# The first norm's sum of squares moved from GpSimd to ScalarE, and the first operands read from PSUM

## The chip, the cores and the metric

One Trainium2 chip, one core of it. The metric is the time of one execution on the device in microseconds (us); lower is better. A core has TensorE (matrix multiplication), VectorE and GpSimd (elementwise work), ScalarE (elementwise functions) and SyncE, which here only issues DMA transfers. In the profile they are PE (PEld for its weight loads), DVE, POOL, ACT and SP.

## The reference

One layer of a decoder for 512 tokens of 1024 features, all in float32: a half-step gated feed-forward, two attention mixers with a gated merge, a second half-step feed-forward, a last norm. The change lies in the first feed-forward alone:

```
def _rmsnorm(x, g):
    xf = x.astype(jnp.float32)
    y = xf * lax.rsqrt(jnp.mean(xf * xf, axis=-1, keepdims=True) + RMS_EPS)
    return (y * g.astype(jnp.float32)).astype(x.dtype)

def _swiglu(x, w_gate, w_up, w_down):
    return (jax.nn.silu(x @ w_gate) * (x @ w_up)) @ w_down
...
    h = x
    ...
        h = h + FFN_HALF * _swiglu(_rmsnorm(h, norm_ffn1[i]), ffn1_gate[i], ffn1_up[i], ffn1_down[i])
```

`x` is 512 x 1024, the gate and up weights are 1024 x 2816, the down weights 2816 x 1024.

## The kernel before, in words

**Operands in two parts.** Every large product is made of three matmuls of 128x128 weights with 512 moving columns. A float32 operand is split into a high part, rounded by ScalarE (`uh` for activations, `whi` for weights), and a low part, what the rounding left, subtracted by VectorE (`ul`, `wlo`). The product is whi·uh + whi·ul + wlo·uh, summed in one bank of PSUM.

**Layout.** Activations lie with features on partitions: `h[:, d]` is the d-tile, 128 features by 512 tokens; there are eight, numbered 0 to 7 here. The input comes with tokens on partitions (`x`, four blocks of 128 tokens), so TensorE first transposes four 128x128 blocks of each tile into a bank `tp`. There are two such banks, used in turn.

**The norm's factor is applied late.** The matmuls take h times the gain, without the token's factor 1/sqrt(mean of squares). The factor, `r_b`, is worked out beside them, and multiplies the products afterwards (`swiglu`). `norm_in` makes uh and ul of a tile and calls `square`, in which GpSimd adds the tile's squares to `sqacc`. `norm_col` sums `sqacc` over partitions by matmuls with a column of ones and turns the sums into factors (`nv`, `ny`, `nb`, `rcol`); `norm_rows` spreads them over partitions into `r_b`.

**The start.** For the first two f-tiles (128 columns of gate and of up each), four products run along while the input arrives: `begun` holds four PSUM banks, named o, s, acc and o by the profile, and `begin(f, m, d)` adds tile d's three matmuls to one of them (f the f-tile, m gate or up). `x_in(d)` makes a tile: transposes, the copy to `h[:, d]` on VectorE, `norm_in`, and the split of the tile's rows of these first weights (`w_in0`) into `W.hi` and `W.lo`, 128x512. Each engine works its instructions in the order of the code; that order is written by hand here: x_in(0), x_in(1), then in turn the twelve matmuls of tile d and x_in(d + 2). At the end come tiles 6 and 7, with nine matmuls of tile 6 (three banks) before those of tile 7.

**After it.** Later weights come in blocks of 128 columns, eight k-tiles deep, into four slots; `W.next` splits a block two ahead of its use (`high` on ScalarE, `low` on VectorE). Blocks 0, 1, 2 go to the slots that the start used. `mm3` is a block's 24 matmuls; at three quarters of the first block's it calls `col` (that is, `norm_col`), in the second's `rows`.

Of the kernel before, what the change touches and what calls it, by code (L numbers as in the profile page):

```python
# [16 lines left out]
D = 1024  # L17
# [21 lines left out]
def parts(x):  # L39
    """x as three parts of eight bits, whose products with 16-bit integers are exact in float32, and a rest."""  # L40
    out = []
    for _ in range(3):
        m, e = math.frexp(x)
        c = math.ldexp(round(m * 256), e - 8)
        out.append(c)
        x -= c
    return out + [x]
# [11 lines left out]
class Weights:  # L59
    """Streams 128-column blocks of weights from DRAM and splits them into a high and a low part."""  # L60
# [49 lines left out]
    def prep_pair(self):  # L110
        """The next two blocks, by halves of their rows."""
# [16 lines left out]
    def next_pair(self):  # L128
        """Two blocks side by side, as [128, 2, 8, 128]."""
        i = self.pos  # L130
        assert i % 2 == 0
        self.prep(i + 1 + self.AHEAD)
        self.pos += 2
        s = i % self.SLOTS
        return self.hi[:, s:s + 2], self.lo[:, s:s + 2]
# [10 lines left out]
def cols(w, width, r0, nk, c0, n):  # L146
    """Rows r0..r0+128*nk, columns c0..c0+n of a [rows, width] matrix, as [128, nk, n]."""
# [3 lines left out]
class Ring:  # L151
    """n buffers, used in turn."""
# [16 lines left out]
class Task:  # L169
    """A few instructions of one engine: emit() issues them. It takes a buffer of some rings and gives back others."""  # L170
# [6 lines left out]
class Schedule:  # L177
    """Orders tasks by a list schedule: whatever can start first, and the lower rank first where several can."""
# [7 lines left out]
    def add(self, us, emit, after=(), take=(), give=(), rank=0):  # L186
        """us: the engines that can do it, with their estimated microseconds."""
# [40 lines left out]
def layer(ctx, tc, a, out):  # L228
# [27 lines left out]
    # ---- the order in which the weights are used  # L256
# [45 lines left out]
    # ---- constants  # L302
# [46 lines left out]
    def rope_tables(p):  # L349
        """Cosines and sines of position x inverse frequency, for any int32 position: the angle is brought to  # L350
        [-pi, pi] by multiples of 2 pi and of 65536 that are exact in parts."""
# [51 lines left out]
    # ---- norms  # L403
    def norm_in(d, norm):
        """The d-tile of the normed input without the token's factor, in two parts; its sum of squares."""
# [13 lines left out]
    def norm_col():  # L419
        """1 / sqrt(mean of squares + eps), with tokens on partitions."""  # L420
        ps = tbank()
        for t in range(4):
            mm(ps[:, 0, t:t + 1], sqacc[:, t * 128:(t + 1) * 128], ones[:, :1], True, True)
        v = temp.tile([128, 4], F32, name="nv", bufs=1)
        vector.tensor_scalar(v, ps[:, 0, :4], 1.0 / D, EPS, op0=OP.mult, op1=OP.add)
# [19 lines left out]
    # ---- feed-forward  # L445
# [23 lines left out]
    def ffn(after, begun=(), side=None, finish=None):  # L469
        """begun: gates and ups of the first f-tiles; after(d): when a d-tile is done; side: small pieces of other  # L470
        work, one for each f-tile; finish: the last third's products with the down weights, in another way."""
        norm = {}

        def col():
            norm["col"] = norm_col()
# [29 lines left out]
    # ---- first feed-forward  # L505
    hd = tc.dram_tile([KD, 128, S], F32, name="hd")

    with pool("h1") as h_pool, pool("temp1", 2) as temp, pool("start") as start:
# [22 lines left out]
        def rows_in(n):  # L531
            """The first n rows, as columns."""
# [8 lines left out]
        def x_in(d):  # L541
# [3 lines left out]
            vector.tensor_copy(h[:, d], flat(ps))  # L545
            norm_in(d, 0)
            src = w_in0[:, d].rearrange("p m (f c) -> p f m c", f=2)
            hi, lo = (w[:, :, d].rearrange("p (f m) c -> p f m c", f=2) for w in (W.hi, W.lo))
            scalar.copy(hi, src)
            vector.tensor_tensor(lo, src, f32(hi), op=OP.subtract)  # L550

        def begin(f, m, k):
            s = 2 * f + m
            mm(begun[f][m], W.hi[:, s, k], uh[:, k], k == 0, False)
            mm(begun[f][m], W.hi[:, s, k], ul[:, k], False, False)
            mm(begun[f][m], W.lo[:, s, k], uh[:, k], False, k == KD - 1)
# [4 lines left out]
        for d in range(KD - 2):  # L561
            for f in range(2):
                for m in range(2):
                    begin(f, m, d)
            x_in(d + 2)
        W.load(2)
        load_rest()
        for f, m, d in ((0, 0, 6), (0, 1, 6), (1, 0, 6), (0, 0, 7), (0, 1, 7), (1, 0, 7), (1, 1, 6), (1, 1, 7)):
            begin(f, m, d)
# [20 lines left out]
        ffn(to_mix, begun, side_work())  # L590

    # ---- mixers
    with ExitStack() as mixing:
# [16 lines left out]
        # places that are used for other things before the attention needs them  # L610
# [11 lines left out]
        # -- the first projection, as the input gets ready; keys and values that will be compressed  # L622
# [29 lines left out]
        # -- everything up to the merge: a list schedule of small tasks  # L652
# [14 lines left out]
        def either(us):  # L667
            """An elementwise step on SBUF that VectorE does in us microseconds, or GpSimd."""
# [4 lines left out]
        def prepare(first, n):  # L673
            """Tasks that split the blocks first.., by halves of their rows."""
# [35 lines left out]
        class Bank:  # L710
            """A PSUM bank, taken when its first task is issued."""
# [6 lines left out]
        def project(done):  # L718
            """256 columns of the input projection with tokens on partitions; done(t0, bank, task) for each bank."""
# [17 lines left out]
        def rope(src, t0, nt, nh):  # L737
            """src [128, nt, nh, 64] turned by the tables of the tokens of t0.., and times the token's factor: two
            parts, to be added."""
# [10 lines left out]
        class Turned:  # L750
            """What rope leaves, between its task and the next ones."""
# [13 lines left out]
        # where a rotated or transposed operand is complete  # L765
# [655 lines left out]
```

## Time and profile before

| | |
|---|---|
| median of 3 timed runs | 1151.49 us (1151.38 to 1151.9) |
| span of the profiled execution, first to last instruction | 1146.2 us |
| median less that span | 5.3 us |
| TensorE busy | 1119.1 us, 98% of the span |
| VectorE busy | 661.4 us, 58% |
| ScalarE busy | 436.9 us, 38% |
| GpSimd busy | 151.6 us, 13% |
| granted TensorE clock, mean | 0.997 of full speed |

The profile gives a span for the profiled execution and no other time of it; what lies around the span is taken from the median. The shares are means over stages with different limits: TensorE is busy for 98% of the span, but for 31 of the first 40 us (4.95 in the first ten, 26.33 in the next thirty).

### The profile page before, as it was taken

Reading aid. Unit: us, or ns where it says so; the run is one execution under the profiler, and the core shown is the slowest. Engines: PE = TensorE matmul, PEld = TensorE weight load, DVE = VectorE, ACT = ScalarE, POOL = GpSimd, SP = SyncE. Lnnn points to the kernel's source line nnn. Section 1 sums busy time; section 2 is a strip of 40 time slices with the busy share of each in tenths; the row PEclk is TensorE's granted clock in tenths of the full one; section 3 lists DMA queues with packets and bytes.
Section 4 is the critical chain, followed back from the end, with each engine's and each line's share of the span. In section 5 each row is a group of like instructions: output and inputs, shape, how many; then the busy total and the mean of one; then the engine's idle time right before and its main releaser. Section 6 shows DMA issues by size and latency. Waiting matters only on the chain.

```text
span 1146.2 us, 14637 instructions
## 1 busy us (share of the span) xinstructions
PE 1119.1 (98%) x5591; PEld 940.1 (82%) x5591; DVE 661.4 (58%) x1227; ACT 436.9 (38%) x850; POOL 151.6 (13%) x152
## 2 busy tenths in 40 slices
PE   7999999999999999999999899999999999999997
PEld 5788888888888899888888688888888888888875
DVE  6665336443446689999889644565443354433453
ACT  3333123221233356767777533323232132222432
POOL 5300000000004321422121222241000000000001
PEclk9999999999999999999999999999999999999999
DMA  7233333333324533242211255433333333333221
GB/s 226 74 111 92 95 96 89 108 99 108 88 82 130 156 88 98 74 112 72 59 38 37 82 149 147 138 92 111 110 100 97 97 91 94 109 93 92 74 74 74
DMA packets 198287, 113.34 MB, mean 99 GB/s; under 512 B 4996, under 2 KB 191944, under 8 KB 198216
## 3 DMA queue, kind: packets, MB, share of 16 engines
q1 hardware_dynamic: 197416, 111.33, 34.0%
q8 instruction: 44, 0.72, 0.3%
q10 hardware_dynamic: 800, 1.07, 0.3%
q14 instruction: 27, 0.22, 0.1%
HBM read 105.83 MB, written 6.55 MB: 98 GB/s over the span
## 4 chain that ended last, share of the span: by engine, by line
PE 86%; DVE 8%; ACT 1%; issue 1%; POOLq 0%; DVEq 0%; ACTq 0%
PE acc L250 31%; PE s L250 27%; PE o L250 24%; DVE wlo L97 2%; PE tp L1224 2%; DVE s L1130 1%; DVE pts L1239 1%; PE tp L250 1%; DVE osum L1267 0%; DVE pbuf L1161 0%; PE tp L850 0%; DVE h L501 0%; DVE pbuf L1159 0%; PE tp L1345 0%; ACT whi L93 0%
## 5 line engine op out<-in xcount | busy, mean ns | idle before, releaser
L97 DVE TENSOR_TENSOR wlo<-raw,whi 128x1024 fp32r<-128x1024 f32 (+3 forms) x221 | 242.6, 1127 | 28.4 <-ACT whi L93 27.3
L93 ACT CAST whi<-raw 128x1024 fp32r<-128x1024 f32 (+3 forms) x223 | 189.8, 890 | 132.7 <-PE acc L250 53.1
L250 PE MATMUL acc<-uh,whi 128*128 128x512 f32 x296 | 116.9, 395 | 0.0
L250 PE MATMUL acc<-uh,wlo 128*128 128x512 f32 x296 | 115.8, 391 | 0.0
L250 PE MATMUL acc<-ul,whi 128*128 128x512 f32 x296 | 115.4, 390 | 0.0
L250 PE MATMUL s<-uh,whi 128*128 128x512 f32 x280 | 109.5, 391 | 0.0
L250 PE MATMUL s<-ul,whi 128*128 128x512 f32 x280 | 109.2, 390 | 0.0
L250 PE MATMUL s<-uh,wlo 128*128 128x512 f32 x280 | 109.2, 390 | 0.0
L250 PE MATMUL o<-uh,wlo 128*128 128x512 f32 x256 | 100.6, 393 | 3.7 <-DVE wlo L550 3.7
L250 PE MATMUL o<-uh,whi 128*128 128x512 f32 x256 | 101.0, 394 | 0.0
L250 PE MATMUL o<-ul,whi 128*128 128x512 f32 x256 | 100.0, 391 | 0.0
L253 ACT CAST G<-g 128x512 fp32r<-128x512 f32 x44 | 27.3, 621 | 186.7 <-DVE g L466 186.7
L250 PE MATMUL acc<-G,whi 128*128 128x512 f32 x280 | 87.5, 394 | 0.0
L250 PE MATMUL s<-G,whi 128*128 128x512 f32 x228 | 70.3, 390 | 0.0
L250 PE MATMUL o<-G,whi 128*128 128x512 f32 x228 | 70.2, 389 | 0.0
L250 PE MATMUL acc<-whi,uh 128*128 128x256 f32 x224 | 64.7, 289 | 2.1 <-DVE v L809 2.1
L250 PEld LDWEIGHTS acc<-uh,wlo 128*128 128x128 f32 x296 | 55.6, 188 | 12.2 <-DVE wlo L97 0.4
L250 PE MATMUL acc<-wlo,uh 128*128 128x256 f32 x224 | 63.6, 284 | 1.6 <-DVE wlo L97 1.6
L250 PEld LDWEIGHTS acc<-uh,whi 128*128 128x128 f32 x296 | 55.8, 188 | 10.8 <-issue 0.2
L250 PEld LDWEIGHTS acc<-ul,whi 128*128 128x128 f32 x296 | 55.7, 188 | 10.6
L462 ACT ACTIVATE s<-z 128x512 f32<-128x512 f32 x44 | 27.9, 633 | 95.2 <-DVE z L460 95.2
L250 PE MATMUL acc<-whi,ul 128*128 128x256 f32 x224 | 63.3, 283 | 0.0
(291 smaller groups left out, 2140.2 us busy)
## 6 DMA issues: line engine op xcount, KB each, us to landing
raw<-in_ffn_gate_dram SPq DMA_DIRECT2D x42, 512.0 KB, 4.0
raw<-in_ffn_up_dram SPq DMA_DIRECT2D x42, 512.0 KB, 5.0
raw<-in_ffn_down_dram SPq DMA_DIRECT2D x38, 512.0 KB, 4.5
raw<-in_w_in_dram SPq DMA_DIRECT2D x32, 512.0 KB, 4.6
raw<-in_w_out_dram SPq DMA_DIRECT2D x8, 512.0 KB, 4.2
raw<-in_ffn_down_dram SPq DMA_DIRECT2D x8, 384.0 KB, 4.1
zd<-turn_a SPq DMA_DIRECT2D x9, 256.0 KB, 2.1
z<-zd SPq DMA_DIRECT2D x9, 256.0 KB, 2.8
```

The costliest lines, as they stand in the source:

```text
L93: self.nc.scalar.copy(self.place(i)[0][:, k0:k1], self.raw[i][:, k0:k1])
L97: engine.tensor_tensor(lo, self.raw[i][:, k0:k1], f32(hi), op=OP.subtract)
L250: tensor.matmul(out, lhsT, rhs, start=start, stop=stop)
L253: scalar.copy(hi, src)
L462: scalar.activation(s, z, AF.Silu)
L1130: vector.tensor_tensor_reduce(b.view[:, j], b.view[:, j], u.mask, 1.0, u.least(hd), OP.add, OP.min, u.m[:, hd:hd + 1])
L1224: tensor.transpose(ps[:w, hd], u.p[:, hd, kb * w:kb * w + w], ident)
L1239: vector.tensor_tensor(p.lo, flat(b.ps)[:w], f32(p.hi), op=OP.subtract)
```

## The change

In the first feed-forward, the sum of squares is no longer taken from `h` on GpSimd but from the input `x`, with tokens on partitions, by four ScalarE activations (Square, with the sum of each row), one for each block of 128 tokens. `col_of` turns those sums into factors; the matmuls with a column of ones fall away for this norm. `uh` and `ul` are made from the transposed tile in PSUM, and the copy to `h` follows them. The order of the matmuls of `begin` is by operand: first whi·uh for all banks, then whi·ul, then wlo·uh. For tiles 6 and 7 the first f-tile's two banks come first, then the other two. In tile 0 the weights are rounded ahead of uh.

```diff
     def norm_col():
         ps = tbank()
         for t in range(4):
             mm(ps[:, 0, t:t + 1], sqacc[:, t * 128:(t + 1) * 128], ones[:, :1], True, True)
+        return col_of(ps[:, 0, :4])
+
+    def col_of(sums):
         v = temp.tile([128, 4], F32, name="nv", bufs=1)
-        vector.tensor_scalar(v, ps[:, 0, :4], 1.0 / D, EPS, op0=OP.mult, op1=OP.add)
+        vector.tensor_scalar(v, sums, 1.0 / D, EPS, op0=OP.mult, op1=OP.add)
...
-            norm["col"] = norm_col()
+            norm["col"] = norm_col() if sums is None else col_of(sums)
...
         def x_in(d):
             ps = tbank()
             for t in range(4):
                 tensor.transpose(ps[:, t], x[:, t, d * 128:(d + 1) * 128], ident)
-            vector.tensor_copy(h[:, d], flat(ps))
-            norm_in(d, 0)
+            g = gains[:, 0, d:d + 1]
             src = w_in0[:, d].rearrange("p m (f c) -> p f m c", f=2)
             hi, lo = (w[:, :, d].rearrange("p (f m) c -> p f m c", f=2) for w in (W.hi, W.lo))
-            scalar.copy(hi, src)
-            vector.tensor_tensor(lo, src, f32(hi), op=OP.subtract)
-
-        def begin(f, m, k):
-            s = 2 * f + m
-            mm(begun[f][m], W.hi[:, s, k], uh[:, k], k == 0, False)
-            mm(begun[f][m], W.hi[:, s, k], ul[:, k], False, False)
-            mm(begun[f][m], W.lo[:, s, k], uh[:, k], False, k == KD - 1)
+            if d == 0:
+                scalar.copy(hi, src)
+            scalar.activation(uh[:, d], flat(ps), AF.Identity, scale=g)
+            if d:
+                scalar.copy(hi, src)
+            if d == 0:
+                vector.tensor_tensor(lo, src, f32(hi), op=OP.subtract)
+            vector.scalar_tensor_tensor(ul[:, d], flat(ps), g, f32(uh[:, d]), op0=OP.mult, op1=OP.subtract)
+            if d:
+                vector.tensor_tensor(lo, src, f32(hi), op=OP.subtract)
+            vector.tensor_copy(h[:, d], flat(ps))
+
+        sums0 = start.tile([128, 4], F32, name="sums0")
+        x_sq = start.tile([128, D], F32, name="x_sq")
+
+        def sum_squares(t):
+            scalar.activation(x_sq, x[:, t], AF.Square, accum_out=sums0[:, t:t + 1])
+
+        PAIRS = [(f, m) for f in range(2) for m in range(2)]
+
+        def begin(pairs, k):
+            for n in range(3):
+                for f, m in pairs:
+                    s = 2 * f + m
+                    w = (W.hi, W.hi, W.lo)[n][:, s, k]
+                    mm(begun[f][m], w, (uh, ul, uh)[n][:, k], k == 0 and n == 0, k == KD - 1 and n == 2)
 
         x_in(0)
         x_in(1)
         vector.tensor_copy(ident_r, ident)
         for d in range(KD - 2):
-            for f in range(2):
-                for m in range(2):
-                    begin(f, m, d)
+            begin(PAIRS, d)
             x_in(d + 2)
+            if d >= 2:
+                sum_squares(d - 2)
         W.load(2)
         load_rest()
-        for f, m, d in ((0, 0, 6), (0, 1, 6), (1, 0, 6), (0, 0, 7), (0, 1, 7), (1, 0, 7), (1, 1, 6), (1, 1, 7)):
-            begin(f, m, d)
+        for pairs, d in ((PAIRS[:2], 6), (PAIRS[:2], 7), (PAIRS[2:], 6), (PAIRS[2:], 7)):
+            begin(pairs, d)
...
-        ffn(to_mix, begun, side_work())
+        ffn(to_mix, begun, side_work(), sums=sums0)
```

VectorE's order at tiles 2 and 3, before (the number behind a name tells buffers apart; `tp_173` and `tp_198` are the transposed tiles 2 and 3):

```order
L545 COPY h_108<-tp_173 128x512
L408 SCALAR_TENSOR_TENSOR ul_75<-h_108,cols_c_86,uh_74 128x512
L550 TENSOR_TENSOR wlo_71<-w_in0_112,whi_70 128x4x128
L545 COPY h_108<-tp_198 128x512
L408 SCALAR_TENSOR_TENSOR ul_75<-h_108,cols_c_86,uh_74 128x512
L550 TENSOR_TENSOR wlo_71<-w_in0_112,whi_70 128x4x128
```

The same place in the changed kernel, where `tp_171` and `tp_193` are tiles 2 and 3:

```order
L558 SCALAR_TENSOR_TENSOR ul_75<-tp_171,cols_c_86,uh_74 128x512
L560 TENSOR_TENSOR wlo_71<-w_in0_112,whi_70 128x4x128
L561 COPY h_108<-tp_171 128x512
L558 SCALAR_TENSOR_TENSOR ul_75<-tp_193,cols_c_86,uh_74 128x512
L560 TENSOR_TENSOR wlo_71<-w_in0_112,whi_70 128x4x128
L561 COPY h_108<-tp_193 128x512
```

The copy has moved from the head of a tile to its end, and ul has another source.

ScalarE's order in the changed kernel for tiles 6 and 7 and the first blocks of later weights (before, the same rows without the two Squares):

```order
L553 ACTIVATE uh<-tp,cols_c 128x512
L555 CAST whi<-w_in_112 128x4x128
L567 ACTIVATE x_sq,sums_136<-x 128x1024
L553 ACTIVATE uh<-tp,cols_c 128x512
L555 CAST whi<-w_in_112 128x4x128
L567 ACTIVATE x_sq,sums_136<-x 128x1024
L93 CAST whi<-raw 128x1024 x4
```

A Square stands behind each of tiles 4 to 7, the last of them ahead of the rounding of block 0.

TensorE's order at tiles 6 and 7, before: the first three rows are tile 6's for the first bank, the last three tile 7's for the same bank.

```order
L250 MATMUL o_132<-uh_74,whi_70 128x512
L250 MATMUL o_132<-ul_75,whi_70 128x512
L250 MATMUL o_132<-uh_74,wlo_71 128x512
L250 MATMUL s_133<-uh_74,whi_70 128x512
L250 MATMUL s_133<-ul_75,whi_70 128x512
L250 MATMUL s_133<-uh_74,wlo_71 128x512
L250 MATMUL acc_134<-uh_74,whi_70 128x512
L250 MATMUL acc_134<-ul_75,whi_70 128x512
L250 MATMUL acc_134<-uh_74,wlo_71 128x512
L250 MATMUL o_132<-uh_74,whi_70 128x512
L250 MATMUL o_132<-ul_75,whi_70 128x512
L250 MATMUL o_132<-uh_74,wlo_71 128x512
```

The same place in the changed kernel, six rows of tile 6 and six of tile 7:

```order
L250 MATMUL o_132<-uh_74,whi_70 128x512
L250 MATMUL s_133<-uh_74,whi_70 128x512
L250 MATMUL o_132<-ul_75,whi_70 128x512
L250 MATMUL s_133<-ul_75,whi_70 128x512
L250 MATMUL o_132<-uh_74,wlo_71 128x512
L250 MATMUL s_133<-uh_74,wlo_71 128x512
L250 MATMUL o_132<-uh_74,whi_70 128x512
L250 MATMUL s_133<-uh_74,whi_70 128x512
L250 MATMUL o_132<-ul_75,whi_70 128x512
L250 MATMUL s_133<-ul_75,whi_70 128x512
L250 MATMUL o_132<-uh_74,wlo_71 128x512
L250 MATMUL s_133<-uh_74,wlo_71 128x512
```

Six matmuls of tile 6 stand ahead of tile 7's first, where nine did, and each operand is asked for two matmuls at a time. The other twelve of the two tiles follow.

## Rows read from the trace of the kernel before

**Rows 1.** The page's first line.

```profile
span 1146.2 us, 14637 instructions
```

**Rows 2.** Chain that ended last, 0 to 70: start us, us, engine, tile, line.

```profile
39.02 4.08 PE s L250 x18
```

**Rows 3.** Waits, 0 to 60: who waited for whom, us in total, times, longest.

```profile
PEld o L250 <- DVE wlo L550: 6.4, 7, 1.5
```

**Rows 4.** Timeline: start us, us, engine, line, operation, out<-in, [idle before <-releaser].

```profile
11.58 0.48 PE L250 MATMUL o<-uh,whi 128*128 128x512 f32 x1
...
13.77 1.61 POOL L417 TENSOR_TENSOR sqacc<-sqacc,turn_a 128x512 f32<-128x512 f32 x1
...
14.16 1.77 DVE L550 TENSOR_TENSOR wlo<-w_in,whi 128x512 fp32r<-128x512 f32 x1
...
14.77 0.48 PE L250 MATMUL o<-uh,whi 128*128 128x512 f32 x1
...
15.86 0.68 DVE L545 COPY h<-tp 128x512 f32<-128x512 f32 x1
15.99 0.50 PE L250 MATMUL o<-uh,wlo 128*128 128x512 f32 x1 [0.51 <-DVE wlo L550]
...
30.64 0.48 PE L250 MATMUL o<-uh,whi 128*128 128x512 f32 x1
```

**Rows 5.** VectorE's groups, 10 to 36: count | busy us, mean ns | idle before, releaser.

```profile
L550 DVE TENSOR_TENSOR wlo<-w_in,whi 128x512 fp32r<-128x512 f32 x7 | 12.4, 1770 | 0.0
L408 DVE SCALAR_TENSOR_TENSOR ul<-h,cols_c,uh 128x512 fp32r<-128x512 f32 x7 | 6.1, 874 | 5.5 <-ACT uh L407 5.5
```

**Rows 6.** VectorE's groups, 0 to 10.

```profile
L550 DVE TENSOR_TENSOR wlo<-w_in,whi 128x512 fp32r<-128x512 f32 x1 | 0.7, 677 | 0.0
```

**Rows 7.** ScalarE's groups by form, whole span.

```profile
L549 ACT CAST whi<-w_in 128x512 fp32r<-128x512 f32 x8 | 4.8, 604 | 0.0
...
L443 ACT COPY r_b<-tp 128x512 f32<-128x512 f32 x3 | 1.8, 587 | 27.4 <-PE tp L250 27.4
```

**Rows 8.** ScalarE's groups by form, 1100 to 1146 (L1377 Square, L1389 Identity).

```profile
L1377 ACT ACTIVATE z<-o_t 128x512 f32<-128x512 f32 x8 | 5.1, 632 | 19.0 <-DVE o_t L1375 19.0
L1389 ACT ACTIVATE o_t<-o_t,fcol 128x512 f32<-128x512 f32 x4 | 2.9, 724 | 6.5 <-DVE fcol L1387 6.5
...
L1377 ACT ACTIVATION_READ_ACCUMULATOR z<-o_t 128x1 f32 x8 | 1.5, 185 | 0.0
```

**Rows 9.** Timeline, tile 7's low part and the blocks behind it.

```profile
35.78 0.50 PE L250 MATMUL o<-uh,wlo 128*128 128x512 f32 x1 [1.19 <-DVE wlo L550]
35.80 4.08 ACT L93 CAST whi<-raw 128x1024 fp32r<-128x1024 f32 x4 [2.16 <-issue]
...
36.88 3.50 DVE L97 TENSOR_TENSOR wlo<-raw,whi 128x1024 fp32r<-128x1024 f32 x3 [1.16 <-ACT whi L93]
...
38.86 0.39 PE L250 MATMUL s<-uh,whi 128*128 128x512 f32 x1
```

**Rows 10.** Timeline, around the matmuls with ones.

```profile
42.71 0.39 PE L250 MATMUL s<-uh,wlo 128*128 128x512 f32 x1
...
43.75 0.49 PE L250 MATMUL s<-uh,whi 128*128 128x512 f32 x1
```

**Rows 11.** Timeline, the start.

```profile
1.44 1.28 ACT L407 ACT_TABLE_LOAD   x1 [1.44 <-PEq L1409]
...
6.25 0.60 ACT L549 CAST whi<-w_in 128x512 fp32r<-128x512 f32 x1
...
6.41 1.09 PE L544 MATMUL tp<-ident,x 128*128 128x128 f32 x4 [1.55 <-DMA x<-in_x_dram]
...
7.14 0.78 PE L250 MATMUL o<-uh,whi 128*128 128x512 f32 x1
```

**Rows 12.** Tile w_in, the first gate weights' DMA, issued at 1.28.

```profile
DMA to landing us min/median/max: 2.8/2.8/2.8
```

**Rows 13.** Busy us by stretch (count); last columns granted clock, DMA share, GB/s.

```profile
645.00:646.00 1.00, 1.00 (x4) 0.81 (x4) 0.28 (x1) 0.58 (x1) 0.95 (x1) 0.50 0.00 0
```

More of the change, by code (lines that the diff above doesn't have):

```diff
@@ L467, in swiglu, with ffn @@
         split(G[:, j], G[:, 8 + j], g)
-    def ffn(after, begun=(), side=None, finish=None):
+    def ffn(after, begun=(), side=None, finish=None, sums=None):
         norm = {}
         def col():
-            norm["col"] = norm_col()
+            norm["col"] = norm_col() if sums is None else col_of(sums)
         def rows():
@@ L1064, in layer @@
         class Unit:
+            pass
         def nsa_units(g, order=range(4)):
```

## The prediction

> **What bounds the kernel now.** The profiled execution spans 1146.2 us [rows 1]; the timed runs have their median at 1151.49, so 5.3 us lie outside the span, and I carry them over unchanged. I read the chain of waits first. From 35.7 us on it is TensorE almost without a break, in stretches such as 18 matmuls in 4.08 us, 0.227 us for each [rows 2]. So whatever TensorE wins or loses early moves everything behind it, unless something later has a clock of its own. The list of waits of the first 60 us then says where TensorE is not yet the bound: its weight loads waited seven times, 6.4 us together, for the low part wlo of the first weights, which VectorE makes [rows 3]. The timeline of tiles 1 to 7 shows how [rows 4]. From the first matmul of tile 1 (11.58) to that of tile 2 (14.77) is 3.19 us: twelve matmuls and four transposes without a stall. Then tile 2's third matmul stands until 15.99. From 14.77 to 30.64, the first matmul of tile 6, four tiles take 15.87 us, 3.97 each.
>
> Why 3.97? VectorE is one loop: copy h (0.68), wait for ScalarE's uh, which reads that copy (0.80), ul (0.87), wlo (1.77), next copy. In the timeline the copy for tile 3 begins at 15.86, where wlo of tile 2 ends [rows 4]. And wlo is long: 1770 ns for each of seven [rows 5], but 677 ns for the one before 10 us [rows 6]. GpSimd is in its 1.61 us addition into sqacc when the long one starts at 14.16; that addition ends at 15.38, and wlo 0.55 us later [rows 4]. So I read wlo as held up by that addition, and the loop as made of three things that the change touches.
>
> **What the change does, part by part.** *GpSimd's fifteen instructions (one product, seven products, seven additions) go.* Nobody else waits for GpSimd there except the first normalization. wlo then should cost its undisturbed 0.68. Bounds: 0.68 [rows 6] and, if GpSimd is not the cause, 1.77 [rows 5]. I take 0.68.
>
> *uh and ul read PSUM, the copy h comes last.* ScalarE no longer waits for VectorE. uh from PSUM has no row; nearest are ScalarE's 587 ns copy of a bank to r_b [rows 7] and the 724 ns of an Identity with a scale column from SBUF [rows 8]; I take 0.72. ul from PSUM has no row either; I take today's 0.87 [rows 5]. VectorE per tile, with the copy of 0.68 [rows 4], is then 0.87 + 0.68 + 0.68 = 2.23 us, against the 3.19 that TensorE needs; ul could double and still fit. The bank of the transposes is held until the copy, but the next transposes into it come two tiles later. ScalarE per tile is 0.72 + 0.60 = 1.32 [rows 7].
>
> *Four Squares of 128x1024 on ScalarE, one behind each of tiles 4 to 7.* Two rows of 128x512 bound one from above: 2 x 0.632 + 0.185 for reading the accumulator = 1.45 [rows 8]; below, a single one with its read, 0.82. I take 1.45. ScalarE then needs 2.77 a tile, still under 3.19, so a Square may take up to 1.87 and stay hidden. What hides it is TensorE's own work. What waits behind the last Square is the rounding of weight block 0.
>
> Does Square need other tables than Identity? The change's instruction order has one table load at the start and none around the Squares, and in the last 46 us of today's span Square runs beside Identity [rows 8], with no table load among ScalarE's groups. The Trainium skill, "ScalarE: Activation LUTs", section "What ACT_TABLE_LOAD costs", puts every switch to another set at about 2.66 us, and its section "Table sets: the hidden batching unit" says that cheap functions stand in every set, without naming Square among them. No run here shows that figure; the trace has 1.28 us for a load [rows 11]. If two loads went with each Square, that page's price would make an estimated 1163; the sum below has none.
>
> *The steady tiles.* With both engines under 3.19, four periods of 3.97 become 3.19: 15.87 - 12.76 = 3.11 us won.
>
> *Tiles 6 and 7.* Tile 7's transposes are still issued just before tile 6's first matmul, so tile 7 is made in the shadow of tile 6's share. Before, that share was nine matmuls, and tile 7's third matmul still came only at 35.78; from 30.64 to block 0's first matmul at 38.86 went 8.22 us for 24 matmuls [rows 4, 9]. Now six matmuls (1.36 us) go first, then tile 7's, by operand: uh and whi are due 0.72 + 0.60 and some 0.2 of handing over after the transposes, so TensorE waits some 0.3; ul and wlo (0.87 + 0.68 behind uh, 2.3 in all) are due as two pairs of matmuls are done, 2.3 to 2.6. 24 x 0.227 = 5.45, plus 0.3, makes 5.75: 2.47 us won. Bounds of the wait: 0 and 0.6.
>
> *Block 0 behind it.* Today its rounding starts at 35.80, as tile 7's wlo ends, four take 4.08 on ScalarE, and three subtractions 3.50 on VectorE [rows 9]. In the new order it stands behind the last Square, about 1.6 + 1.45 = 3.1 us after tile 7's transposes; 1.02 of rounding and 1.17 of subtraction end at 5.3 to 5.5. TensorE wants the rounded part at 5.75 and the low part two matmuls later, at 6.2. It fits with some 0.7 us to spare, so I charge nothing; if the cover goes, each us beyond costs one.
>
> *The sum over partitions on TensorE.* The matmuls with a column of ones stood between two matmuls at 42.71 and 43.75 [rows 10]: 1.04 in place of 0.227, 0.81 us won. The rest of that chain (power, products, r_b) starts earlier; SyncE's queue keeps its order.
>
> *The grouping by operand.* Every matmul loads its weights as before; a group of four gives ul and wlo two more steps of time. I cost it at nothing.
>
> *The start.* Now the first table load waits for the first gate weights, issued at 1.28 and landed 2.8 us later [rows 12], at 4.1; plus 1.28, 0.60, 0.72 gives uh at 6.7, before tile 1's transposes, which wait for x until 6.41, let the first matmul go at 7.14 [rows 11]. When the up weights land no row says, but the cast that needs them began at 6.25 [rows 11]: at worst uh is 0.5 late. I take 0, bounds -0.15 (a gap between the first two matmuls) and +0.5.
>
> **Sum:** 3.11 + 2.47 + 0.81 = 6.4 us. The span goes to 1139.8, the time to **1145.1** (-0.56%).
>
> **Rivals.** *wlo stays at 1.77,* because something other than GpSimd stretches it. Against it stands the short one [rows 6]. VectorE then needs 0.87 + 1.77 + 0.68 = 3.32 a tile, 0.13 over TensorE, 0.5 in four tiles, and tile 7's low part comes 1.1 later: 1146.7.
>
> *Late start,* up weights at 6.25: 1145.6.
>
> *A later wait that goes or comes.* At 645 to 648 us three windows of 1 us ran at granted clock 0.50, four matmuls each [rows 13], the lower of the two levels (1.2 GHz), after a stretch of short pieces of attention. If the shifted timeline spares it, 1.5 us more are won: 1143.6. A second one would give 1146.6.
>
> *ScalarE becomes the bound through longer Squares,* without tables: beyond 1.87 each, four times the excess is lost. At 2.9, 4.1 us would go, and 1149.2 is left, a gain of 0.2%, which is about what a measurement of this kernel can tell from no change.
>
> *Square and Identity take turns in the tables.* Two loads of 1.28 [rows 11] make a Square 1.45 + 2.57 = 4.0. Tiles 5 to 7 and block 0 each come 4.0 - 1.87 = 2.15 late, 8.6 in all, of which about 1.4 is cover (tile 5's operands are ready that much ahead of need): 7.2 lost, 1152.3, slower than before; from 1.5 us a switch on it is slower by over 0.2%. The instruction order, with one load, and the end of today's span [rows 8] speak against it. The Trainium skill's price for a switch, on the page named above, lies beyond that point.
>
> **Chances.** The forecast 0.65; late start 0.12; wlo unchanged 0.10; the clock stretch spared 0.05; longer Squares 0.05; tables 0.03. The low end is the spared stretch with 0.3 for the spread of runs, 1143.3; the high end wlo unchanged with the same, 1147.0; both reach over the bounds of the start and of tile 7's wait. What lies outside is the last two cases and mishaps that I did not think of. Faster by over 0.2%: 0.92; within: 0.05; slower: 0.03.
>
> **What the changed profile would show.** No GpSimd work before the power step; all wlo of the first eight tiles near 0.68; first matmuls of tiles 2 to 6 each 3.19 apart, with the first of tile 6 near 27.5; block 0's first matmul near 33.3; no matmul with ones and sqacc between 42 and 44 less the shift; Squares of 1.2 to 1.45 with no table load beside them. The prediction is wrong if tiles still come over 3.4 apart, if ScalarE turns up as the releaser of TensorE's waits in tiles 5 to 7 for more than 1 us, if block 0 waits for its rounding, or if the 5 to 6 us won by 40 us are not there any more at the end.

## The result, and the profile after

The changed kernel took 1142.88 us (median of 4 runs, 1142.62 to 1143.16), the kernel before 1151.43 us beside it (4 runs, 1147.91 to 1151.9): ratio 0.9929, 95% interval 0.9915 to 0.9943. The direction was right; the time lies 0.4 us below the range's low end and 2.2 us below the forecast. The same kernel, run again later (e5 below), took 1146.55 us (7 runs, 1142.94 to 1146.66). Both are times of one program, and most of this text is about why they differ.

The page's first line and its busy times answer to [rows 1]:

```profile
span 1141.3 us, 14617 instructions
...
PE 1117.3 (98%) x5583; PEld 939.8 (82%) x5583; DVE 652.8 (57%) x1227; ACT 440.9 (39%) x858; POOL 132.1 (12%) x137
```

The profiled execution took 1143.02 us, 1.7 us more than its span. That is the first thing that does not fit the prediction, which put 5.3 us outside the span.

TensorE's timeline, the first matmuls of tiles 0, 1, 2, 6 and 7 and of block 0 (start, duration, in brackets the idle time before and who ended it), beside [rows 4, 9, 11]:

```profile
8.07 0.80 PE L250 MATMUL o<-uh,whi 128*128 128x512 f32 x1 [0.62 <-ACT uh L553]
...
10.37 0.63 PE L250 MATMUL s<-ul,whi 128*128 128x512 f32 x1
10.80 0.63 PE L250 MATMUL acc<-ul,whi 128*128 128x512 f32 x1
...
13.04 0.48 PE L250 MATMUL o<-uh,whi 128*128 128x512 f32 x1
...
16.23 0.48 PE L250 MATMUL o<-uh,whi 128*128 128x512 f32 x1
...
29.08 0.48 PE L250 MATMUL o<-uh,whi 128*128 128x512 f32 x1
...
30.61 0.50 PE L250 MATMUL o<-uh,whi 128*128 128x512 f32 x1
...
34.86 0.39 PE L250 MATMUL s<-uh,whi 128*128 128x512 f32 x1
```

From 16.23 to 29.08 four tiles take 12.85 us, 3.21 each, where they took 15.87: 3.02 won. From tile 6 to block 0 it is 5.78 where it was 8.22: 2.44 won. But tile 0 starts at 8.07 instead of 7.14, and from there to tile 1 it is 4.97 instead of 4.44 (11.58 - 7.14), since from one matmul to the next it is 0.4 us or more eight times, not six, as from 10.37 to 10.80: 0.93 + 0.53 = 1.46 lost. In the trace of before the slow pace ended with these two:

```profile
9.43 0.57 PE L250 MATMUL s<-uh,wlo 128*128 128x512 f32 x1
9.84 0.39 PE L250 MATMUL acc<-uh,whi 128*128 128x512 f32 x1
```

With the ones matmuls' 0.81, 3.02 + 2.44 + 0.81 - 1.46 = 4.81, against 1146.2 - 1141.3 = 4.9 between the two spans.

ScalarE's timeline shows why tile 0 is late, beside [rows 11]:

```profile
5.52 1.28 ACT L552 ACT_TABLE_LOAD   x1 [5.52 <-DMA w_in<-in_ffn_up_dram]
6.81 0.62 ACT L552 CAST whi<-w_in 128x512 fp32r<-128x512 f32 x1
7.34 1.26 ACT L553 ACTIVATE uh<-tp,cols_c 128x512 fp32r<-128x512 f32 x2
```

The table load stood at 1.44 before. Now the first activation in ScalarE's order is the cast of the weights, the load stands in front of it, and what the load waits for is the up weights' DMA, until 5.5.

VectorE's groups from 11 to 36 us (count | busy us, mean ns | idle before, releaser), beside [rows 5]:

```profile
L561 DVE COPY h<-tp 128x512 f32<-128x512 f32 x7 | 4.8, 685 | 0.0
L558 DVE SCALAR_TENSOR_TENSOR ul<-tp,cols_c,uh 128x512 fp32r<-128x512 f32 x6 | 4.5, 751 | 8.9 <-ACT uh L553 8.9
L560 DVE TENSOR_TENSOR wlo<-w_in,whi 128x512 fp32r<-128x512 f32 x6 | 4.1, 682 | 0.0
```

ScalarE's groups of the first 45 us, beside [rows 7, 8]:

```profile
L553 ACT ACTIVATE uh<-tp,cols_c 128x512 fp32r<-128x512 f32 x8 | 5.4, 687 | 11.1 <-PE tp L547 11.1
...
L567 ACT ACTIVATE x_sq<-x 128x1024 f32<-128x1024 f32 x4 | 4.3, 1064 | 0.0
...
L552 ACT ACT_TABLE_LOAD x1 | 1.3, 1283 | 5.5 <-DMA w_in<-in_ffn_up_dram 5.5
L567 ACT ACTIVATION_READ_ACCUMULATOR x_sq<-x 128x1 f32 x4 | 0.8, 189 | 0.0
```

wlo is 682 ns instead of 1770, a Square with its read 1.25 us, and there is one table load. Of the waits of the first 60 us (us in total, times, longest), the 6.4 us of [rows 3] are gone. These remain of the weight loads' waits for high and low parts; the middle one is at 58.5 us, in a later block, and the last is tile 7's:

```profile
PEld o L250 <- ACT uh L553: 1.0, 1, 1.0
...
PEld acc L250 <- DVE wlo L97: 0.4, 1, 0.4
PEld o L250 <- ACT whi L555: 0.3, 1, 0.3
```

### The profile page after: what moved, and what is told of

It reads as the page before. It is cut to its first block, busy times and chain, and to the rows that moved or that the text cites. A ratio compares the mean times of both kernels' runs of the same rounds, so it can differ in the third digit from the quotient of the medians.

```text
span 1141.3 us, 14617 instructions
## 1 busy us (share of the span) xinstructions
PE 1117.3 (98%) x5583; PEld 939.8 (82%) x5583; DVE 652.8 (57%) x1227; ACT 440.9 (39%) x858; POOL 132.1 (12%) x137
## 4 chain that ended last, share of the span: by engine, by line
PE 88%; DVE 8%; issue 1%; ACT 1%; DMA 0%; SPq 0%; POOLq 0%; DVEq 0%; ACTq 0%
PE acc L250 32%; PE s L250 28%; PE o L250 25%; DVE wlo L97 2%; PE tp L1244 2%; DVE s L1150 1%; DVE pts L1259 1%; PE tp L250 0%; DVE osum L1287 0%; DVE pbuf L1181 0%; PE tp L870 0%; DVE h L504 0%; DVE pbuf L1179 0%; DMA w_in<-in_ffn_up_dram 0%; PE tp L1365 0%
```

## Experiments

Twelve kernels ran, two of them unaltered: e1 to e4 on one chip, e5 to e8 on a second, e9 to e12 on a third, each time with the kernel before beside them. Before took 1151.03 (17 runs, 1148.06 to 1152.63), 1151.39 (18, 1147.96 to 1152.11) and 1149.24 us (17, 1147.84 to 1152.48) there, and the ratios are against these. Every run's time was 1.7 or 1.8 us over its span.

### e1, e5: both kernels unaltered

> The kernel before, unchanged, against itself. Its first three timed runs were at 1151.4 to 1151.9 us and a later one at 1147.91, and its profiled span of 1146.2 with the 1.7 us that lie between span and time in each run of the changed kernel makes 1147.9. Theory A, the program has two durations: both 1147.9 and 1151.5 turn up among these runs, about 3.5 us apart, and the spans differ by as much, so that part of the measured gain is that the changed kernel always takes the shorter one. Rival, the first three runs belong to other circumstances (another chip, for one) and here all runs lie within 1 us of each other, near 1147.9; then the true gain is about 5 us, not 8.5.

Measured: 1151.57 us (12 runs, 1148.59 to 1152.46), ratio 1.0002 (0.9992 to 1.0012). The profiled run took 1150.93 and spans 1149.2 us, 3.0 more than the span of [rows 1] for the same program. Theory A holds, but with more than two durations; the rival does not.

> The changed kernel, unaltered. Theory A (the prediction's base failed, since executions of one program differ by 1.7 or 3.4 us of half-clock stretches that lie inside the span): its executions spread too, over some 1141 to 1146 us, in groups 1.7 us apart, every profiled time is 1.7 us over its span, and its shortest stands about 6 us under the shortest of before (1148.1). Rival (the change itself took the long executions away): all executions lie within 0.6 us, at 1142.6 to 1143.2.

Measured: 1146.55 us (7 runs, 1142.94 to 1146.66), ratio 0.9962 (0.9947 to 0.9977); the profiled run took 1146.23, its span is 1144.5. Theory A holds in that the runs spread and the time over the span is 1.7; the shortest is 5.0 under the shortest of before beside it (1147.96), not 6. The rival does not hold. Windows of 1 us in e5's trace (busy us of each engine with counts; the last three columns are granted clock, DMA share, GB/s):

```profile
460.00:461.00 1.00, 0.98 (x4) 1.00 (x5) 1.00 (x3) 1.00 (x4) 0.00 (x0) 0.50 1.15 323
461.00:462.00 1.00, 1.00 (x7) 1.00 (x6) 0.96 (x5) 1.00 (x4) 0.00 (x0) 0.50 0.96 224
...
645.00:646.00 1.00, 1.00 (x4) 0.81 (x3) 0.00 (x0) 0.99 (x2) 0.00 (x0) 0.50 0.04 10
```

The same windows in the trace of the changed kernel's first run:

```profile
460.00:461.00 1.00, 1.00 (x11) 1.00 (x10) 1.00 (x2) 1.00 (x4) 0.00 (x0) 1.00 1.04 268
...
641.00:642.00 1.00, 1.00 (x4) 0.81 (x3) 0.58 (x2) 0.38 (x1) 0.00 (x0) 0.50 0.00 0
...
645.00:646.00 1.00, 1.00 (x6) 0.81 (x6) 1.00 (x1) 0.95 (x2) 0.07 (x1) 1.00 0.25 92
```

The same program at the same place: 4 and 7 matmuls in a us at granted clock 0.50 (1.2 GHz), or 11 at 1.00 (2.4 GHz). In e5 the windows from 460 to 463 and from 641 to 647 read 0.50, in the first run only those from 640 to 643. Ahead of the first stretch TensorE had been idle for 2.06 us in e5 and for 2.05 in the run that kept its clock, waiting both times for VectorE's `v`. The row of e5 comes first, that of the first run second:

```profile
460.02 0.55 PE L250 MATMUL acc<-whi,uh 128*128 128x256 f32 x1 [2.06 <-DVE v L829]
...
459.49 0.36 PE L250 MATMUL acc<-whi,uh 128*128 128x256 f32 x1 [2.05 <-DVE v L829]
```

Each run also lists its mean granted clock, and that separates the short from the long executions of both kernels:

| mean granted clock of the run | before: runs, median (range) | after: runs, median (range) | difference |
|---|---|---|---|
| 0.997 | 15, 1148.14 (1147.84 to 1149.02) | 5, 1142.94 (1142.62 to 1143.16) | 5.2 |
| 0.996 | 13, 1150.79 (1149.08 to 1151.71) | 1, 1145.68 | 5.1 |
| 0.995 | 6, 1149.55 (1149.24 to 1149.69) | none | |
| 0.993 | 30, 1151.70 (1151.28 to 1152.63) | 5, 1146.56 (1146.23 to 1146.66) | 5.1 |

(The column of before holds the runs beside the three groups and those of e1; that of after the first four runs and e5.) The traces show what stands behind the levels. At 0.997 (the two first traces and e8) only the second place has half clock, for some three windows; at 0.993 (e2, e4, e5) the first place has it for some three and the second for six. Between them the mean is no exact label: e1, at 0.996, has three windows at each place, e6, at 0.996 too, six at the second alone, as e3 has at 0.995. At 0.997 and at 0.993 the change is worth 5.2 and 5.1 us; the row at 0.996 has a single run of the changed kernel and shows little. The first comparison, 8.5 us between the medians, set four runs of the changed kernel that all lay at 0.997 against a median of before at the level of 0.993.

### e6, e7: TensorE kept busy in the idle stretch ahead of the products at 464 (after: 459) us

```diff
                         mm(ps, blk[ix][:, r * 8 + i], lo[:, :, i], False, i == 7)
+                    if (ix, r, j) == (1, 0, 6):
+                        for _ in range(16):
+                            mm(b.ps[:, 256:], blk[ix][:, 7], hi[:, :, 7], True, True)
```

> The kernel before, with 16 matmuls more (1.9 us, into the unused half of a bank) where TensorE stood idle for 2.06 us ahead of the products that start at 464.4 us. Theory A, in its part on this idle: no window of half clock between 462 and 472 us in the trace, and the executions at 1151.5 to 1152.6 become rare: median 1149.5 to 1150.5, lowest still about 1148. Rival (the clock falls there for another reason, or the spread comes from other places): median and range as before, 1151.0 and 1148 to 1152.6.

Measured: 1149.46 us (12 runs, 1148.53 to 1150.13), ratio 0.9988 (0.998 to 0.9997). The sixteen matmuls and what follows them in its timeline:

```profile
462.72 2.08 PE L250 MATMUL acc<-whi,G 128*128 128x256 f32 x16
464.95 0.36 PE L250 MATMUL acc<-whi,uh 128*128 128x256 f32 x1
```

No window from 459 to 471 reads below 1.00, no run is above 1150.13, where 13 of the 18 runs of before were, and the median falls by 1.9. The stretch at 642 to 649 is still there. The theory holds. Doing more work lowered the median; the lowest run, 1148.53, is 0.6 over the lowest of before beside it (1147.96), so what is won is the long executions.

> The changed kernel with the same 16 matmuls in the same idle (2.05 us, ahead of the products at 459.5 us). Theory A: no half clock between 457 and 467 us, and no execution above 1144; median 1141.5 to 1143. Rival: the spread of the changed kernel unaltered, median within 0.3 us of it.

Measured: 1143.94 us (6 runs, 1142.42 to 1144.83), ratio 0.9942 (0.9928 to 0.9957), 2.6 under e5 on the same chip. No half clock between 457 and 467 us, as expected; the median and the highest run are 0.9 and 0.8 above what was expected, and the trace has half clock from 638 to 644.

### e9, e11: both places filled

Beside the edit of e6, ten matmuls into a free bank of PSUM, in the four idle stretches of 0.5 to 0.9 us between 635 and 640 us, three in each of the first two and two in each of the others (`KEEP` says how many at which call):

```diff
+        def busy(what):
+            n = KEEP.get((what, calls[what]), 0)
+            if n:
+                ps = psum.tile([128, 512], F32, name="acc")
+                for _ in range(n):
+                    mm(ps, uh[:, 0, :128], uh[:, 0], True, True)
...
                         mm(o, u.v(kb), p.hi, kb == 0 and u.first, False)
+                        busy("v")
```

> The changed kernel with TensorE kept busy in both places: the 16 matmuls of the variant before, and ten matmuls into a free bank in the four idle stretches between 635 and 640 us (0.9 us each). Theory (the half-clock stretches follow idle stretches of TensorE): no half clock at 457 to 467 nor at 637 to 650 us, all executions between 1139.5 and 1141.7, that is 1.7 to 3.4 us under the variant with the first filling alone (1142.4 to 1144.8). Rival (the stretch at 640 has another cause, or the added matmuls lie in the way): half clock there still, times as with the first filling alone or longer.

Measured: 1141.80 us (6 runs, 1141.51 to 1143.17), ratio 0.9931 (0.9917 to 0.9945). Its windows at the place where [rows 13] read 0.50:

```profile
640.00:641.00 1.00, 1.00 (x5) 0.81 (x6) 0.36 (x1) 0.54 (x1) 0.93 (x2) 1.00 0.00 0
641.00:642.00 1.00, 1.00 (x6) 0.82 (x5) 0.52 (x3) 0.46 (x2) 0.58 (x1) 1.00 0.00 0
```

Half clock is gone from both places, and the median falls by another 2.1 (on another chip). It is 0.1 above what was expected, and one run is 1.4 higher: something else still varies, the start among it, as shown below. Only the end of the trace still has half clock, as the end of every trace here has.

> The kernel before with both fillings, so that neither of the compared kernels has half-clock stretches: its distance to the changed kernel with both fillings is the worth of the change alone. By the spans of the two first traces it is 4.9 us (1146.2 - 1141.3), by the prediction's sum 6.4 us. Theory: executions at 1144.5 to 1146.8, median 4.5 to 5.3 us over the changed kernel with both fillings; rival (the sum was right and the spans misleading): 6.2 to 6.6 us over it.

Measured: 1147.60 us (12 runs, 1146.49 to 1148.09), ratio 0.9981 (0.9971 to 0.9991); no half clock at either place. Over e9 that is 5.8 us by the medians, 5.0 by the lowest runs, 5.5 by the spans (1145.5 and 1140.0). It falls between theory and rival, above the 5.3 that I had as the theory's end and under the sum's 6.4. By the two timelines the steady tiles are 2.97 apart, the tail 2.53, tile 2's first matmul comes 1.08 later in e9, and with the ones' 0.81 that makes 5.2. The rest of the medians' 5.8 is not accounted for.

### e3, e4: one half of the change each

e3 takes before, with the Squares in place of GpSimd's squares and of the ones matmuls, and keeps its copies, its order and its operands:

```diff
-        square(d)
+        if norm:
+            square(d)
...
             x_in(d + 2)
+            if d >= 2:
+                sum_squares(d - 2)
```

> The kernel before with only the sum of squares moved to ScalarE's Squares (the matmuls with ones gone, no GpSimd work in the first tiles); uh and ul still read h, the copy still goes first, matmuls in the old order. Theory (GpSimd's addition is what stretches wlo): wlo falls to 0.68 us, VectorE's loop to 0.68 + 0.80 + 0.87 + 0.68 = 3.0, under TensorE's 3.19, and the tiles come 3.2 apart as in the changed kernel; with the ones gone and a somewhat shorter tail some 5 us under the kernel before, and no late start. Rival (it is the reading of PSUM that frees the loop): wlo stays near 1.8 or the tiles stay near 3.9 apart, and only the 0.8 us of the matmuls with ones are won.

Measured: 1143.21 us (5 runs, 1142.68 to 1143.81), ratio 0.9934 (0.9922 to 0.9946). VectorE's groups from 10 to 36 us:

```profile
L408 DVE SCALAR_TENSOR_TENSOR ul<-h,cols_c,uh 128x512 fp32r<-128x512 f32 x7 | 5.3, 751 | 5.5 <-ACT uh L407 5.5
L554 DVE TENSOR_TENSOR wlo<-w_in,whi 128x512 fp32r<-128x512 f32 x7 | 4.8, 684 | 0.0
```

Tiles 2 to 6 come 3.21 apart (15.29 to 28.12), tile 6 to block 0 takes 6.26, and the first matmul stands at 7.78. The theory holds: taking GpSimd's work away is enough for the steady tiles. The reads of PSUM and the new order give another 0.5 us in the tail, but in the changed kernel's trace tile 2 stood 0.94 later than here. In the time the two cancel: at clock 0.997 e3's three runs have their median at 1142.88, the five of the changed kernel at 1142.94. As far as these runs tell, moving the squares alone is worth as much as the whole change.

e4 takes after, with `square(d)` at the end of `x_in` again, the ones matmuls back, and no Squares.

> The changed kernel with the sum of squares on GpSimd as before (fifteen GpSimd instructions, matmuls with ones back, no Squares); operands from PSUM, copy last, matmuls by operand as in the change. Theory (GpSimd's addition stretches whatever VectorE does on two SBUF operands): wlo stays near 1.77, VectorE needs about 0.75 + 1.77 + 0.68 = 3.2 a tile, just TensorE's 3.2, so the tiles come 3.2 to 3.4 apart, tile 7's low part is about 1 us later and the ones cost 0.8: some 2 to 3 us slower than the changed kernel, still faster than before by 2 to 3. Rival (wlo was stretched by something else that the change removed): wlo near 0.7, and only the 0.8 us of the ones separate it from the changed kernel.

Measured: 1145.45 us (6 runs, 1144.08 to 1147.95), ratio 0.9954 (0.9941 to 0.9967). VectorE's groups from 10 to 36 us:

```profile
L560 DVE TENSOR_TENSOR wlo<-w_in,whi 128x512 fp32r<-128x512 f32 x7 | 7.3, 1048 | 0.0
L558 DVE SCALAR_TENSOR_TENSOR ul<-tp,cols_c,uh 128x512 fp32r<-128x512 f32 x7 | 5.2, 750 | 7.5 <-ACT uh L553 7.5
```

Here too the tiles come 3.21 apart (17.56 to 30.42). wlo took neither the 1.77 of the theory nor the rival's 0.7: its mean of 1.05 is made of four at 1.10 to 1.54, which began while GpSimd was well inside an instruction, and three at 0.68, which did not. Two pairs of its timeline:

```profile
22.16 1.29 POOL L417 TENSOR_TENSOR sqacc<-sqacc,turn_a 128x512 f32<-128x512 f32 x1
22.45 1.54 DVE L560 TENSOR_TENSOR wlo<-w_in,whi 128x512 fp32r<-128x512 f32 x1
...
25.67 0.68 DVE L560 TENSOR_TENSOR wlo<-w_in,whi 128x512 fp32r<-128x512 f32 x1
25.79 1.70 POOL L417 TENSOR_TENSOR sqacc<-sqacc,turn_a 128x512 f32<-128x512 f32 x1
```

Where GpSimd's instruction began first, wlo ended 0.54 or 0.55 us after it, as in [rows 4] (0.55); where wlo began ahead of the addition, it took 0.68 and the addition 1.70. With the mean, 1.05 + 0.75 + 0.68 = 2.48 us a tile is under TensorE's need. So either half alone mends the steady tiles; they are not added up. At clock 0.997 e4's three runs have their median at 1144.39, 1.5 over the changed kernel; 0.8 of that is the ones.

### e8: the grouping by operand undone

```diff
-            for n in range(3):
-                for f, m in pairs:
+            for f, m in pairs:
+                for n in range(3):
```

> The changed kernel with each bank's three products together again at the start (the grouping by operand undone, the reads of PSUM kept). Theory (the grouping costs and gives nothing): first matmuls of tiles 2 to 6 still 3.2 us apart, and 5.8 us from tile 6's first to block 0's first; time as the changed kernel within 0.3 us. Rival (the order gives the half microsecond by which the variant with the sums alone was longer in the last two tiles): 6.2 to 6.3 us there, 0.5 us more in the time.

Measured: 1144.97 us (6 runs, 1144.15 to 1147.53), ratio 0.9959 (0.9943 to 0.9975). At clock 0.997 its three runs lie at 1144.15 to 1144.40, 1.2 to 1.5 above the 1142.94 of the unaltered kernel. Two rows of its timeline, tile 6 and block 0:

```profile
30.00 0.48 PE L250 MATMUL o<-uh,whi 128*128 128x512 f32 x1
...
36.17 0.39 PE L250 MATMUL s<-uh,whi 128*128 128x512 f32 x1
```

6.17 us instead of 5.78 (5.77 in e5), while tiles 2 to 6 stay 3.21 apart: the rival, nearly. The grouping is worth 0.4 us in the tail and nothing in the steady tiles. Another 0.9 stands ahead of tile 2 (17.15 against 16.23), where slow matmuls went on to 13.0 us. Part of that is the order: between the first three matmuls lie 0.80 and 0.59 us instead of 0.59 and 0.43, since the second one now wants ul, and e8's list of waits up to 15 us has

```profile
PEld o L250 <- DVE ul L558: 0.5, 1, 0.5
```

That is some 0.4 us, as much as e8 is behind e5 at tile 2 (16.79). The other 0.5 is a later first matmul (8.22) and more slow ones, which vary with the order unchanged too.

### e2, e10, e12: the start

e2 takes after, with two lines that call for the table early, behind the first DMA that ScalarE issues:

```diff
+        early = start.tile([128, 4], F32, name="early")
+        scalar.copy(early, mhalf)
```

> The changed kernel with a 4-column copy on ScalarE right after its first DMA issue, so that the table load no longer waits for the first weights. Theory (late start): the first matmul comes back from 8.07 to about 7.1 to 7.3 us, and the step to the full clock comes earlier with it, so that tile 2's first matmul is near 14.8 again instead of 16.23, block 0's near 33.4, and the time about 1.4 us under the changed kernel's. Rival (the step to the full clock does not follow the first matmul): the first matmul comes 0.9 us earlier, but the clock steps up at 11.9 as before, the matmuls done by then are simply two more at the lower level, and about 0.4 us is won. Second rival: the start was not what counted, no difference.

Measured: 1144.04 us (6 runs, 1141.74 to 1145.55), ratio 0.9935 (0.992 to 0.9951). ScalarE's timeline starts with

```profile
1.44 1.28 ACT L519 ACT_TABLE_LOAD   x1 [1.44 <-PEq L1431]
2.74 0.19 ACT L519 COPY early<-mhalf 128x4 f32<-128x4 f32 x1
```

The load is back at 1.44, the first matmul at 7.39, but the matmuls stayed 0.43 us apart until 11.8, and tile 2 came at 15.89, 0.34 earlier than in the changed kernel's first trace: the rival's picture. That compares two single executions, though. Against e5, which has the same clock of 0.993, tile 2 comes 0.90 earlier, and the times at equal clock say 1.0 to 1.1: medians of 1141.97 (three runs at 0.997) and 1145.43 (three at 0.993) against 1142.94 and 1146.56. e10 is e9 with the same two lines:

> The same with the table load early as well. Theory: 0.3 us under the variant with both fillings, by the 0.34 us by which the early load alone brought tile 2's first matmul forward; first matmul at 7.4 instead of 8.0 to 8.3. Rival (the second weights' load or the clock at the start takes it back): within 0.1 us of it.

Measured: 1140.63 us (5 runs, 1140.27 to 1141.52), ratio 0.9921 (0.9905 to 0.9936). 1.2 under e9, four times what I had expected from e2's trace and about what e2's times show. In this execution the slow matmuls ended at 9.6, and tile 2 came at 14.87. e12 is e10 with eight transposes of the identity while TensorE waits for the first pieces of x:

```diff
             ps = tbank()
+            for _ in range((3, 5)[d] if d < 2 else 0):
+                tensor.transpose(ps[:, 0], ident, ident)
```

> The variant with both fillings and the early table load, and eight transposes of the identity while TensorE waits for the first two pieces of the input (three at 2.6 to 3.7 us, five at 4.9 to 6.4 us). Theory (the matmuls at the start, 0.43 us apart until 11.9 us, come to 0.23 us apart earlier if TensorE was busy before): the change of pace comes before 10 us, tile 2's first matmul at 14.5 to 15.0 instead of 15.9 us, and the time 0.8 to 1.2 us shorter than without them. Rival (the pace changes at a time of its own): 11.9 us still, time the same within 0.3 us.

Measured: 1139.70 us (5 runs, 1139.12 to 1140.7), ratio 0.9913 (0.9897 to 0.9928). The theory holds. e12's timeline, the added transposes and the first matmuls:

```profile
4.71 1.27 PE L552 MATMUL tp<-ident 128*128 128x128 f32 x5
6.52 1.10 PE L554 MATMUL tp<-ident,x 128*128 128x128 f32 x4 [0.54 <-DMA x<-in_x_dram]
7.29 0.56 PE L253 MATMUL o<-uh,whi 128*128 128x512 f32 x1
7.68 0.40 PE L253 MATMUL s<-uh,whi 128*128 128x512 f32 x1
7.92 0.40 PE L253 MATMUL acc<-uh,whi 128*128 128x512 f32 x1
...
13.78 0.48 PE L253 MATMUL o<-uh,whi 128*128 128x512 f32 x1
```

The matmuls lie 0.23 us apart from the second on; tile 2 comes earlier than expected, 1.1 before e10's, and 0.93 of it is in the time. In each of the other thirteen traces five or more of tile 0's matmuls are 0.4 us or more ahead of the next. This is the fastest version, 0.3% under the changed kernel's best runs and 0.6% under its median in e5.

## Why the prediction was wrong, step by step

**The base failed.** The prediction said that "5.3 us lie outside the span, and I carry them over unchanged". In every run 1.7 to 1.8 us lie outside. The profiled execution of before, with its span of 1146.2, must then itself have taken about 1147.9, a run at 0.997 like the 15 in the table; the other 3.6 us lay inside the spans of other executions, as half-clock stretches. So a sum made in a trace at 0.997 was taken from a median at 0.993. With a worth of 5.1, the base of 1147.9 gives 1142.8 and that of 1151.5 gives 1146.4: the two measured medians of the changed kernel, 1142.88 and 1146.55.

On the base of its own trace the sum would have given 1147.9 - 6.4 = 1141.5, too low. In 1145.1 a base 3.6 too high and a sum 1.3 too large stand against each other, so that it came within 2.2 of the first median is luck; so is it that e5's median lies inside the range. My rival with one more half-clock stretch ends at 1146.6, which is e5's median, but by luck as well: it adds 1.5 to a base whose runs held the longer stretches already, and takes 6.4 off where 5.1 was won. I gave a change of stretches 0.05, as a rarity of the changed kernel, where it is the ordinary spread of both.

**"The start" was mis-sized.** Taken at 0 with bounds of -0.15 and +0.5, it cost 1.46 in the two first traces, and that is the whole error of the sum there: 6.4 - 1.5 = 4.9. 0.93 of it is the late first matmul, since the table load waits for the up weights (5.52) and not for the gate weights alone (4.1 in my working); 0.53 is slow matmuls. How much of that is due to the change can be read from the other traces with the same code up to 450 us:

| trace | first matmul, us | slow matmuls in tile 0 (next one 0.4 us or more behind) | tile 2's first matmul, us |
|---|---|---|---|
| before: first, e1, e6, e11 | 7.14, 7.64, 7.51, 7.67 | 6, 11, 6, 6 | 14.77, 16.39, 15.30, 15.29 |
| after: first, e5, e7, e9 | 8.07, 8.26, 7.99, 8.35 | 8, 10, 11, 7 | 16.23, 16.79, 16.64, 16.37 |

The slow matmuls vary in both kernels, and the first trace of before has the earliest tile 2 of its four. By the means tile 2 comes 1.1 later (15.44, 16.51), and 3.02 + 2.44 + 0.81 - 1.1 = 5.2, the worth at equal clock. That the late load is what costs is shown by taking it away: 1.0 to 1.2 us by the times of e2 and e10.

**"The steady tiles"** 3.11, measured 3.02. **"Tiles 6 and 7"** 2.47, measured 2.44, with the wait of 0.3 for whi as worked out. **"The sum over partitions"** 0.81: the matmuls are gone; in e4, which has them again, they stand at 40.24 us and take the same 1.04 in place of 0.227. **"Block 0 behind it"** 0: its rounding begins at 31.61, and TensorE waits for nothing of it at 34.86. **"The grouping by operand"** 0: right for the steady tiles, 0.4 in the tail by e8, inside a term that I had counted whole, and some 0.4 in tile 0.

**The mechanism** held: wlo at 682 ns, not 1770 (0.68 taken), ul and uh at 0.75 and 0.69 (0.87 and 0.72 taken), Square 1.25 (1.45 taken), no table load beside it. Left unsaid was that either half alone would have done (e3, e4), so "GpSimd's additions" and "reads of PSUM" each explain the same 3 us.

What stays open: why TensorE keeps its clock through an idle stretch of 2.05 us in one execution and loses it in another. With the stretch filled the fall did not come in e6, e7, e9 and e11; what decides it where the stretch is idle they do not show.

## What to carry to other kernels

Set the sum against the time of the execution that the trace comes from, and look at the granted clock of the timed runs before comparing medians: where they differ between two kernels, so do the medians (here by 3.5 us within one program). One trace has one start: a difference there wants several traces or times at equal clock. When an instruction with a late operand becomes the first of ScalarE, see where the table load in front of it goes: here it waited too, and a copy of 0.19 us ahead of it put it back and won 1.0 to 1.2 us. Where TensorE idles for some 2 us in a dense kernel, matmuls without use in the gap can be worth more than they cost: here one such gap gave 1.9 us in the median, and two filled places, the early load and the transposes at the start together took the changed kernel to 1139.70 us, a ratio of 0.9913 to before.

## What the runs showed of the hardware that I had not expected

**The same program has several times.** 64 runs of before, in groups by granted clock, span 4.8 us, 0.4%, twice what I called the measurement's resolution. The traces differ in half-clock stretches at the same two places.

**Slow matmuls at the start vary by execution.** e2 and e10 have the same code up to 450 us; slow matmuls (0.43 us from one to the next) end at 11.8 in one and at 9.6 in the other. The granted-clock column reads 1.00 in those windows, so only the matmuls' spacing (0.43 against 0.23) shows it. The Trainium skill, "TensorE: Matmul & The Clock Gate", section "What's actually happening", says that one kernel shows different counts of slow matmuls at its start from run to run; these traces agree, with ten and five.

**VectorE and GpSimd.** ul with both operands in SBUF took 874 ns beside GpSimd's additions [rows 5] and 751 without them (e3); with one operand in PSUM it took 750 although GpSimd was at work (e4). The Trainium skill, "SBUF — State Buffer", section "Who interferes with whom", has a VectorE instruction with two SBUF inputs contend with GpSimd's reads, and not, outside its two-port modes, one with a single SBUF input. The three numbers agree. In e4 the engine that began first kept its time and the other was held: wlo 0.68 and 1.54 us, the addition 1.70 and 1.29.
